# Down projection of a Strassen feed-forward block: product outermost instead of contraction quarter outermost, with the block sums of W2 made ahead, in the attention stage

## The chip, the cores and the metric

One core of a Trainium2 chip runs the whole encoder layer as one program. The metric is the device time of one execution in microseconds (us), lower is better. The engines are named as in the profile: PE (matmul), PEld (its weight load), DVE (vector), ACT (scalar), POOL (GpSimd) and SP, which in this kernel mostly issues DMAs.

## The reference

The layer is a hybrid mixer (Hyena convolutions and a bidirectional mLSTM), a cross-attention and a feed-forward block, over 2048 tokens of width 1024, in fp32. Only the last two matter here:

```python
h = h + _cross_attention(_rms_norm(h, norm_x_g[l]), _rms_norm(mem, norm_mem_g[l]), ...)
h = h + jnp.square(jax.nn.relu(_rms_norm(h, norm_ff_g[l]) @ ff_w1[l])) @ ff_w2[l]   # 1024 -> 4096 -> 1024
return _rms_norm(h, final_norm_g)
```

## The kernel before

**Stages.** In order of time: the input projection with the Hyena filters, Hyena convolutions and mLSTM scan, interleaved by hand (`weave`, L1850); the attention stage (output projection, scores, softmax, value product, four chunks of 512 tokens), which overlaps the last part of the mLSTM; the up projection; the down projection. `TC_ARGS` (L1837) lets a list scheduler set the order of the instructions on every engine when the program is built: an operation with free buffers and ready inputs can be put ahead of others that stand earlier in the text. The result is one instruction stream per engine, SP's stream of DMA issues among them.

**Arithmetic.** An fp32 product is made of three matmuls of a high and a low part (`mm3`, L339 to L341: high by high, low by high, high by low). Each operand tile of 128x512 is therefore split: ACT copies it to the rounded high part (L1521), DVE or POOL subtracts that from the tile to get the low part (L1522, in `halves`). `raw` (L1514) loads such a tile into a ring of six buffers.

**Strassen.** Up and down projection each use seven block products in place of eight (the Winograd form). In the down projection a block of the result is 512 output columns by 512 tokens. `tp` is one of two pairs of token chunks. The contraction runs over 16 tiles of 128 rows in each half of W2's 4096 rows, so there are 16 values `g` of a 2x2 set of 128x512 blocks of W2 (`blocks_of(2, g)`, L1268). The sums of the activation blocks are written to the DRAM tensor `hc` by the up projection.

**Down projection before (L1777 to L1834).** The loop is over four quarters `o` of the contraction, in each over the seven products in `ORDER_DOWN = (1, 6, 7, 5, 3, 2, 4)`, in each over `tp`, in each over the four tiles `k` of the quarter: 28 products x 2 x 4 = 224 steps of 12 matmuls. After four steps a set of four PSUM banks is added into one of 14 SBUF accumulators (`acc`, L1806; copied at L1804 for three products of the first quarter). Three blocks of W2 per `(o, k)` are loaded to `wring` (`load_w`), two sums are made by `sums_w`, a third and fourth in `fetch_a`; all of this, and the residual (`residual`, L1726), is done beside the matmuls, mostly by POOL. In the last quarter the accumulators are combined into the four result blocks (`add`, L1770, on DVE and POOL), which `turned`, `turn` and `finish` transpose, normalise and store.

**Attention before.** In each of the two loops over eight column tiles per chunk (L1382 and L1474), every odd tile takes one entry of the list `sums` (L1322): 20 empty ones and then four calls of `sums_x`, which load four 256 KB tiles of the residual stream, make four block sums of them on POOL and store these. The rest are made in the up projection. In the same loops POOL adds the squares of each row (`ssum`, L1378), on which the statistics of the softmax depend, and DVE splits every weight tile (L344) and every activation (L351).

Of the kernel before, what the change touches and what calls it, by code (L numbers as in the profile page):

```python
# [133 lines left out]
class Prog:  # L134
# [1161 lines left out]

    def attention(self, es):
# [24 lines left out]
        sums = [None] * 20 + list(range(4))  # L1322
# [39 lines left out]
        for c in range(4):  # L1362
# [19 lines left out]
            for ct in range(8):  # L1382
                yield 5.2
                if ct % 2 == 0:
                    w = next(wst)
                else:
                    k = sums.pop(0) if sums else None
                    if k is not None:
                        self.sums_x(A, k, "sm")
# [84 lines left out]
            for ct in range(8):  # L1474
                yield 5.2
                if ct % 2 == 0:
                    w = next(wst)
                else:
                    k = sums.pop(0) if sums else None
                    if k is not None:  # L1480
                        self.sums_x(A, k, "sm")
# [37 lines left out]
    def halves(self, src, tags, bufs, eng):  # L1519
        hi, lo = (self.R.tile([128, 512], F32R, tag=n, name=n, bufs=bufs) for n in tags)  # L1520
        self.nc.scalar.copy(hi, src)  # L1521
        eng.tensor_tensor(lo, src, hi.bitcast(F32), ALU.subtract)  # L1522
        return hi, lo

    def ffn_open(self, es):
        self.R = es.enter_context(self.tc.tile_pool(name="ring", bufs=1, side="right"))
        self.xt = {}
        self.W, self.WD = {}, {}
# [67 lines left out]
    def ffn(self):  # L1596
# [5 lines left out]
        self.C = self.ctx.enter_context(tc.tile_pool(name="wring", bufs=1))  # L1602
# [4 lines left out]
        def fetch_a(n, k):  # L1607
            o, i = prods[n]
            w = self.blocks_of(2, 4 * o + k)
            eng = nc.vector if n < 6 else nc.gpsimd  # L1610
            if i in (6, 7, 5):
                if i == 6:
                    eng.tensor_tensor(self.WD[k, 0], self.WD[k, 2], self.WD[k, 0], ALU.subtract)
                src = self.WD[k, {6: 0, 7: 1, 5: 2}[i]]
            elif i == 1:
                src = self.WD[k, 0]
            else:
                src = self.raw(w[i == 4][1])
                if i == 3:
                    eng.tensor_tensor(src, src, self.WD[k, 0], ALU.subtract)  # L1620
            aq[n, k] = self.halves(src, ("ah", "al"), 4, eng)

        def load_w(o, k):
            w = self.blocks_of(2, 4 * o + k)
            for j, src in enumerate((w[0][0], w[1][0], w[1][1])):
                t = self.WD[k, j] = self.wtile()
                nc.sync.dma_start(out=t, in_=src)

        def sums_w(k, op=nc.gpsimd.tensor_tensor):
            op(self.WD[k, 2], self.WD[k, 1], self.WD[k, 2], ALU.add)  # L1630
            op(self.WD[k, 1], self.WD[k, 0], self.WD[k, 1], ALU.subtract)

        def fetch_b(s, eng=nc.vector):
            n, tp, k = down[s]
            o, i = prods[n]
            bq[s] = self.halves(self.raw(hc[tp, i - 1, 4 * o + k]), ("bh", "bl"), 6, eng)

        with tc.tile_pool(name="up", bufs=1) as U:
# [23 lines left out]
            for n, (tp, g, i) in enumerate(steps):  # L1662
# [7 lines left out]
                if n + 9 >= len(steps) and n + 5 < len(steps):  # L1670
                    load_w(0, n + 9 - len(steps))
# [40 lines left out]
        with tc.tile_pool(name="down", bufs=1) as B:  # L1712
            acc, ms = {}, []
# [6 lines left out]
            for i in (1, 6, 7, 4, 5, 3, 2):  # L1720
                for tp in range(2):
                    acc[i, tp] = B.tile([128, 4, 512], F32, tag="acc", name="acc", bufs=14)
# [3 lines left out]
            def residual(i, tp, k):  # L1726
                n, h = {2: (0, 0), 7: (1, 1), 3: (1, 0), 4: (0, 1)}[i]
                v = acc[i, tp][:, k]
                nc.sync.dma_start(out=v, in_=h2[2 * tp + n, :, 4 * h + k])
                nc.gpsimd.tensor_tensor(v, v, ms[2 * tp + n], ALU.mult)  # L1730
                if i == 4:
                    nc.gpsimd.tensor_tensor(v, v, acc[7, tp][:, k], ALU.subtract)
# [30 lines left out]
            def turned(c, tp, h, i, j, dst=None):  # L1763
                def one(tag, t):
                    turn(c, h, acc[i, tp], acc[j, tp], t, tag)
                    if dst and t == 3:
                        finish(c, dst)
                return [lambda tag, t=t: one(tag, t) for t in range(4)]

            def add(i, j, tp, eng):  # L1770
                for m in range(4):
                    eng.tensor_tensor(acc[i, tp][:, m], acc[i, tp][:, m], acc[j, tp][:, m], ALU.add)

            early = [(i, tp, k) for i in (7, 4, 3, 2) for tp in range(2) for k in range(4)]
            outs = []
            V, G = nc.vector, nc.gpsimd
            for s, (n, tp, k) in enumerate(down):  # L1777
                o, i = prods[n]
                if n == 0 and tp == 0:
                    sums_w(k, nc.vector.tensor_tensor)  # L1780
                if s + 3 < len(down):
                    fetch_b(s + 3, G if s > 199 and k else V)
                if o < 3 and tp == 0 and i == 2:
                    load_w(o + 1, k)
                if o < 3 and tp == 0 and i == 4:
                    sums_w(k)
                if early and s > 3:
                    residual(*early.pop(0))
# [10 lines left out]
                if k < 3:  # L1799
                    continue  # L1800
                for m in range(4):
                    v = acc[i, tp][:, m]
                    if o == 0 and i in (1, 6, 5):
                        nc.scalar.copy(v, bank[m])  # L1804
                    else:
                        d = nc.vector.tensor_tensor(v, bank[m], v, ALU.add)  # L1806
                        if s + 1 == len(down):
                            tc.keep_in_program_order(d)
                if o < 3:
                    continue  # L1810
                if i == 1:
                    add(2, 1, tp, G)
                elif i == 6:
                    add(6, 1, tp, V)
                elif i == 7:
                    add(7, 6, tp, V)
                    add(3, 6, tp, G)
                elif i == 5:
                    add(3, 5, tp, V)
                    add(5, 7, tp, G)  # L1820
                    add(4, 7, tp, G)
                    if tp:
                        outs += turned(1, 0, 1, 5, 1)
                elif i == 3:
                    c = 2 * tp + 1
                    if not tp:
                        outs += turned(3, 1, 1, 5, 1)
                    outs += turned(c, tp, 0, 3, 6, (acc[6, tp], acc[1, tp]))
                elif i == 2:
                    outs += turned(2 * tp, tp, 0, 2, 7)  # L1830
                elif i == 4:
                    outs += turned(2 * tp, tp, 1, 4, 5, (acc[7, tp], acc[5, tp]))
# [116 lines left out]
```

## Time and profile before

| | us |
|---|---|
| median of 3 runs (lowest, highest) | 3226.48 (3220.32, 3226.53) |
| span of the profiled execution, first to last instruction | 3228.4 |
| attention with the end of the mLSTM | about 1240 to 1945 |
| up projection | about 1945 to 2572 |
| down projection, first to last matmul | 2572.6 to 3210.3 |
| tail: last result block | 3210.3 to 3228.4 |

The page gives the profiled execution no time of its own beside its span, which lies 1.9 us above the median of the runs. Rows of the stretches give their length, then busy time and number of instructions of each engine, the granted TensorE clock, the share of time in which the DMA engines are busy, and GB/s. Rows of the timeline give start, length, engine, line, operation, output and inputs; in square brackets stands how long the engine had been idle, and what released it. Rows of groups give count, busy time, mean ns of one, and the idle time ahead of them.

### The profile page before, as it was taken

The page shows a single profiled execution, that of the slowest core. Times are in us where ns is not written, and L with a number is a line of the kernel's source. Part 1 is how long each engine was busy: PE and PEld are TensorE (multiplying, and loading weights), DVE is VectorE, ACT ScalarE, POOL GpSimd, SP SyncE. Part 2 cuts the span into 40 slices and gives each one's busy share as a digit, 9 for nine tenths or more (in the row PEclk, how much of TensorE's full clock was granted, in tenths as well). Part 3 has the DMA queues.
Part 4 walks back from the last instruction along what each step waited for, and adds up shares of the span by engine and source line. Part 5 has one row for each costly group of instructions (what it writes and reads, how often), then busy time and mean ns, then how long its engine had stood idle before and what let it go on. Part 6 is the DMA issues. An engine that isn't in the chain of part 4 may idle for free.

```text
span 3228.4 us, 45284 instructions
## 1 busy us (share of the span) xinstructions
PE 3059.3 (95%) x15241; PEld 2439.5 (76%) x15241; DVE 2034.9 (63%) x3535; ACT 1502.3 (47%) x2873; POOL 1183.0 (37%) x818
## 2 busy tenths in 40 slices
PE   6999999999999876999999998999999999999998
PEld 5655566776668765898979896888788887888876
DVE  7775366345865755777675547656654676556595
ACT  5533366434764343454454445455555543333335
POOL 0122011100121324223151217776756483434483
PEclk9999999999999997999999999999999999999999
DMA  5564776686687988667384537665644474444434
GB/s 189 190 208 161 252 203 201 178 270 182 185 232 206 287 280 283 184 202 243 121 293 126 175 103 246 214 199 177 200 150 154 154 251 153 137 134 150 124 92 167
DMA packets 451777, 617.98 MB, mean 191 GB/s; under 512 B 39631, under 2 KB 247631, under 8 KB 450521
## 3 DMA queue, kind: packets, MB, share of 16 engines
q1 hardware_dynamic: 415412, 556.57, 55.7%
q10 hardware_dynamic: 36132, 58.51, 5.4%
q8 instruction: 121, 1.98, 0.3%
q14 instruction: 112, 0.91, 0.1%
HBM read 416.73 MB, written 198.21 MB: 190 GB/s over the span
## 4 chain that ended last, share of the span: by engine, by line
PE 51%; DMA 7%; DVE 4%; issue 2%; POOL 2%; ACT 1%; SPq 0%; ACTq 0%; POOLq 0%; DVEq 0%
PE mm L341 11%; PE mm L339 11%; PE mm L340 11%; PE hy L341 5%; PE hy L339 5%; PE hy L340 5%; DMA rw<-rows 1%; DVE bl L1522 1%; DMA va<-vd 1%; PE hy L1205 1%; PE hy L1207 1%; DMA wn<-in_xa_wq_t_dram 1%; DMA wr<-xs 1%; DVE wl L344 0%; PE hy L1443 0%
## 5 line engine op out<-in xcount | busy, mean ns | idle before, releaser
L344 DVE TENSOR_TENSOR wl<-wn,wh 128x512 fp32r<-128x512 f32 (+1 forms) x364 | 283.1, 813 | 119.5 <-ACT wh L344 119.3
L1522 DVE TENSOR_TENSOR bl<-wr,bh 128x512 fp32r<-128x512 f32 x213 | 240.9, 1137 | 124.5 <-ACT bh L1521 122.7
L1521 ACT CAST ah<-w 128x512 fp32r<-128x512 f32 x284 | 176.2, 622 | 298.9 <-PE hy L340 153.4
L921 POOL TENSOR_TENSOR b<-b,a 128x512 f32<-128x512 f32 x64 | 87.7, 1371 | 584.6 <-ACT b L919 461.0
L344 ACT CAST wh<-wn 128x512 fp32r<-128x512 f32 (+1 forms) x364 | 208.4, 618 | 193.6 <-PE mm L340 47.0
L339 PE MATMUL mm<-xh,wh 128*128 128x512 f32 x640 | 270.7, 424 | 5.4 <-ACT xh L499 3.2
L1522 DVE TENSOR_TENSOR al<-w,ah 128x512 fp32r<-128x512 f32 x236 | 221.4, 940 | 60.4 <-ACT ah L1521 60.1
L340 PE MATMUL mm<-xl,wh 128*128 128x512 f32 x640 | 257.0, 402 | 1.8 <-DVE xl L344 1.8
L341 PE MATMUL mm<-xh,wl 128*128 128x512 f32 x640 | 258.3, 404 | 0.0
L1521 ACT CAST bh<-wr 128x512 fp32r<-128x512 f32 x232 | 143.7, 621 | 228.8 <-PE mm L341 183.8
L341 PE MATMUL mm<-bh,al 128*128 128x512 f32 x576 | 225.6, 394 | 7.9 <-DVE al L1522 4.7
L339 PE MATMUL mm<-bh,ah 128*128 128x512 f32 x576 | 227.1, 394 | 0.9 <-DVE u L1647 0.8
L340 PE MATMUL mm<-bl,ah 128*128 128x512 f32 x576 | 226.1, 393 | 0.0
L339 PE MATMUL mm<-act,wh 128*128 128x512 f32 x512 | 199.9, 395 | 3.1 <-ACT wh L344 3.1
L340 PE MATMUL mm<-act,wh 128*128 128x512 f32 x512 | 200.8, 392 | 0.0
L341 PE MATMUL mm<-act,wl 128*128 128x512 f32 x512 | 199.6, 393 | 0.3 <-DVE wl L344 0.3
L1378 POOL TENSOR_TENSOR ssum<-ssum,sq 128x512 f32<-128x512 f32 x56 | 81.9, 1462 | 290.8 <-ACT sq L1377 286.4
L339 PE MATMUL hy<-bh,ah 128*128 128x512 f32 x448 | 175.2, 391 | 0.0
L340 PE MATMUL hy<-bl,ah 128*128 128x512 f32 x448 | 174.6, 390 | 0.0
L341 PE MATMUL hy<-bh,al 128*128 128x512 f32 x448 | 174.4, 390 | 0.0
L339 PEld LDWEIGHTS mm<-xh,wh 128*128 128x128 f32 x640 | 121.4, 190 | 65.7 <-issue 29.7
L339 PE MATMUL hy<-xh,ah 128*128 128x512 f32 x384 | 152.1, 396 | 9.3 <-ACT ah L1521 8.5
(367 smaller groups left out, 8742.1 us busy)
## 6 DMA issues: line engine op xcount, KB each, us to landing
wr<-hc SPq DMA_DIRECT2D x224, 256.0 KB
w<-in_ff_w_dram SPq DMA_DIRECT2D x176, 256.0 KB
hc<-t SPq DMA_DIRECT2D x128, 256.0 KB
wn<-in_w_in_dram SPq DMA_DIRECT2D x100, 256.0 KB
hc<-q SPq DMA_DIRECT2D x96, 256.0 KB
fs<-a SPq DMA_DIRECT2D x32, 512.0 KB
a<-fs SPq DMA_DIRECT2D x64, 256.0 KB
a<-zs SPq DMA_DIRECT2D x64, 256.0 KB
```

The lines of the kernel that those rows point to most:

```text
L339: mm(ps, lh, rh, start=start, stop=False)
L340: mm(ps, lh, rl, start=False, stop=False)
L341: mm(ps, ll, rh, start=False, stop=stop)
L344: both = (self.nc.scalar.copy(hi, src), self.nc.vector.tensor_tensor(lo, src, hi.bitcast(F32), ALU.subtract))
L921: nc.gpsimd.tensor_tensor(xt, xt, hi[:, m], ALU.mult)
L1205: nc.tensor.matmul(dst, nm[:, h], va[:, h], start=True, stop=state is None)
L1207: nc.tensor.matmul(dst, rows_[d, 1][:, h], state[:, h], start=False, stop=True)
L1378: nc.gpsimd.tensor_tensor(ssum, ssum, sq, ALU.add)
L1521: self.nc.scalar.copy(hi, src)
L1522: eng.tensor_tensor(lo, src, hi.bitcast(F32), ALU.subtract)
```

## The change

**Loops.** The down projection loops over the seven products alone, each over `tp`, each over all 16 contraction tiles in one set of four banks (224 steps again). The 14 accumulators are gone: `close` runs after each 16 steps, copies or adds the four banks to at most two running blocks (`m1`, `u2`, `u3`, `c22`, ten buffers with the transposed results), and hands a finished result block to `turned`, whose four parts are taken one every third step.

**Operand A.** Every A tile is loaded by `raw`: blocks 11, 12 and 22 of W2 from the input, the four sums from the DRAM tensor `ws`. The split halves of all 16 tiles stay for both `tp`: four in the old ring, twelve in new tiles `dh` and `dl`. The low part is always made on DVE. `load_w`, the old `sums_w` and the subtractions in `fetch_a` are gone.

**Sums of W2.** A new `sums_w(pool, g)` loads four 256 KB blocks, makes four POOL operations and four 256 KB stores. Its 16 calls are put into the attention's list: `sums` is now 4 empty entries, the 16 calls, and the four `sums_x` in their old place.

```diff
+    def sums_w(self, pool, g):
+        op = self.nc.gpsimd.tensor_tensor
+        ws = self.dram("ws", (4, 16, 128, 512))
+        w = self.blocks_of(2, g)
+        t11, t12, t21, t22 = self.four(pool, [w[m][k] for m in range(2) for k in range(2)], "sm")
+        op(t22, t21, t22, ALU.add)
+        op(t21, t11, t21, ALU.subtract)
+        op(t11, t22, t11, ALU.subtract)
+        op(t12, t12, t11, ALU.subtract)
+        for j, t in enumerate((t22, t11, t21, t12)):
+            self.nc.sync.dma_start(out=ws[j, g], in_=t)
...
-        sums = [None] * 20 + list(range(4))
+        sums = [None] * 4 + [partial(self.sums_w, A, g) for g in range(16)] + [partial(self.sums_x, A, i, "sm") for i in range(4)]
...
-        prods = [(o, i) for o in range(4) for i in self.ORDER_DOWN]
-        down = [(n, tp, k) for n in range(len(prods)) for tp in range(2) for k in range(4)]
+        prods = self.ORDER_DOWN
+        down = [(n, tp, k) for n in range(len(prods)) for tp in range(2) for k in range(16)]
...
+        def fetch_a(n, k, *own):
+            w = self.blocks_of(2, k)
+            src = {1: w[0][0], 2: w[0][1], 4: w[1][1], 5: ws[0, k], 6: ws[1, k], 7: ws[2, k], 3: ws[3, k]}[prods[n]]
+            aq[n, k] = self.halves(self.raw(src), *(own or (("ah", "al"), 4, nc.vector)))
...
+            def close(i, tp, bank, last):
+                def plus(dst, role):
+                    for m in range(4):
+                        d = V.tensor_tensor(dst[:, m], bank[m], T[role, tp][:, m], ALU.add)
...
             for s, (n, tp, k) in enumerate(down):
...
                 if s + 3 < len(down):
-                    fetch_b(s + 3, G if s > 199 and k else V)
+                    fetch_b(s + 3)
+                if n == 0 and tp == 0 and k < 12:
+                    fetch_a(0, k + 4, ("dh", "dl"), 12, V, B)
+                if jobs:
+                    jobs.pop(0)()
...
-                    self.mm3(bank[m], ah[:, msl], al[:, msl], bh, bl, k == 0, k == 3)
+                    self.mm3(bank[m], ah[:, msl], al[:, msl], bh, bl, k == 0, k == 15)
                 if tp and n + 1 < len(prods):
-                    fetch_a(n + 1, k)
-                for _ in range(min(len(outs), 2 if len(outs) > 4 or n + 1 == len(prods) else 1)):
-                    outs.pop(0)("mm" if tp else "hy")
+                    fetch_a(n + 1, k, *((("dh", "dl"), 12, V, B) if k > 3 else ()))
+                if outs and k % 3 == 2:
+                    outs.pop(0)("mm" if tp else "hy")
...
+                if k == 15:
+                    close(prods[n], tp, bank, s + 1 == len(down))
```

More of the change, by code (lines that the diff above doesn't have):

```diff
@@ L1386, in attention @@
                 else:
-                    k = sums.pop(0) if sums else None
-                    if k is not None:
-                        self.sums_x(A, k, "sm")
+                    f = sums.pop(0) if sums else None
+                    if f is not None:
+                        f()
                 if c == 0 and ct == 0:
@@ L1478, in attention @@
                 else:
-                    k = sums.pop(0) if sums else None
-                    if k is not None:
-                        self.sums_x(A, k, "sm")
+                    f = sums.pop(0) if sums else None
+                    if f is not None:
+                        f()
                 if c == 3 and ct == 4:
@@ L1517, in raw, with halves @@
         return t
-    def halves(self, src, tags, bufs, eng):
-        hi, lo = (self.R.tile([128, 512], F32R, tag=n, name=n, bufs=bufs) for n in tags)
+    def halves(self, src, tags, bufs, eng, pool=None):
+        hi, lo = ((pool or self.R).tile([128, 512], F32R, tag=n, name=n, bufs=bufs) for n in tags)
         self.nc.scalar.copy(hi, src)
@@ L1527, in ffn_open @@
         self.xt = {}
-        self.W, self.WD = {}, {}
+        self.W = {}
     def ffn_xload(self, tp, i):
@@ L1669, in ffn @@
                     wq.append(self.ffn_w1(*steps[n + 2]))
-                if n + 9 >= len(steps) and n + 5 < len(steps):
-                    load_w(0, n + 9 - len(steps))
                 if n + 2 >= len(steps):
@@ L1712, in ffn @@
         with tc.tile_pool(name="down", bufs=1) as B:
-            acc, ms = {}, []
+            ms = []
             on = [B.tile([128, D], F32, tag="on", name="on", bufs=2) for _ in range(2)]
@@ L1719, in ffn, with block, residual @@
                     ms.append(v)
-            for i in (1, 6, 7, 4, 5, 3, 2):
-                for tp in range(2):
-                    acc[i, tp] = B.tile([128, 4, 512], F32, tag="acc", name="acc", bufs=14)
             gl = B.tile([128, D], F32, name="gl")
             nc.scalar.dma_start(out=gl, in_=a["final_norm_g"].unsqueeze(0).broadcast_to([128, D]))
-            def residual(i, tp, k):
-                n, h = {2: (0, 0), 7: (1, 1), 3: (1, 0), 4: (0, 1)}[i]
-                v = acc[i, tp][:, k]
+            T = {}
+            def block():
+                return B.tile([128, 4, 512], F32, tag="acc", name="acc", bufs=10)
+            def residual(tp, n, h, role, k):
+                own = role == "c22"
+                v = T[role, tp][:, k] if own else B.tile([128, 512], F32, tag="rs", name="rs", bufs=3)
                 nc.sync.dma_start(out=v, in_=h2[2 * tp + n, :, 4 * h + k])
                 nc.gpsimd.tensor_tensor(v, v, ms[2 * tp + n], ALU.mult)
-                if i == 4:
-                    nc.gpsimd.tensor_tensor(v, v, acc[7, tp][:, k], ALU.subtract)
+                dst = v if own else T[role, tp][:, k]
+                nc.gpsimd.tensor_tensor(dst, v, T["u3", tp][:, k] if own else dst, ALU.add)
             ss = B.tile([128, 4, 2, 4], F32, name="ss")
@@ L1761, in finish, with turned @@
                                 in_=dst[h][:, t - 1:t + 1])
-            def turned(c, tp, h, i, j, dst=None):
+            def turned(tp, n, h, role):
+                c = 2 * tp + n
+                dst = T[h, c] = block()
                 def one(tag, t):
-                    turn(c, h, acc[i, tp], acc[j, tp], t, tag)
-                    if dst and t == 3:
-                        finish(c, dst)
+                    turn(c, h, T[role, tp], dst, t, tag)
+                    if (1 - h, c) in T and t == 3:
+                        finish(c, (T[0, c], T[1, c]))
@@ L1768, in turned, with late @@
                 return [lambda tag, t=t: one(tag, t) for t in range(4)]
[L1770 to L1776, printed above, removed]
+            V = nc.vector
+            jobs, outs = [], []
+            def close(i, tp, bank, last):
+                def plus(dst, role):
+                    for m in range(4):
+                        d = V.tensor_tensor(dst[:, m], bank[m], T[role, tp][:, m], ALU.add)
+                        if last:
+                            tc.keep_in_program_order(d)
+                def late(n, h, role):
+                    jobs.extend(partial(residual, tp, n, h, role, k) for k in range(4))
+                if i == 1:
+                    T["m1", tp] = block()
+                    for m in range(4):
+                        nc.scalar.copy(T["m1", tp][:, m], bank[m])
+                elif i == 6:
+                    T["u2", tp] = block()
+                    plus(T["u2", tp], "m1")
+                    late(0, 0, "m1")
+                elif i == 7:
+                    T["u3", tp] = block()
+                    plus(T["u3", tp], "u2")
+                    T["c22", tp] = block()
+                    late(1, 1, "c22")
+                else:
+                    role = {5: "c22", 3: "u2", 2: "m1", 4: "u3"}[i]
+                    plus(T[role, tp], role)
+                    if i == 5:
+                        plus(T["u2", tp], "u2")
+                        late(1, 0, "u2")
+                        late(0, 1, "u3")
+                    outs.extend(turned(tp, i in (5, 3), i in (5, 4), role))
```

73 lines of the change are left out of this document (3 added, 70 removed).

## The prediction

> **What bounds the kernel now.** First the page, then the stages the change touches, by the table of stretches (length, then busy us and instructions of PE, PEld, DVE, ACT, POOL, the granted clock, the DMA share, GB/s).
>
> ```profile
> PE 3059.3 (95%) x15241; PEld 2439.5 (76%) x15241; DVE 2034.9 (63%) x3535; ACT 1502.3 (47%) x2873; POOL 1183.0 (37%) x818
> ```
> ```profile
> 1240.00:1331.00 91.00, 65.49 (x352) 57.31 (x353) 57.14 (x169) 36.20 (x124) 32.75 (x26) 0.81 0.77 242
> 1331.00:1575.00 244.00, 242.37 (x1636) 222.72 (x1635) 178.22 (x474) 122.72 (x344) 75.69 (x56) 1.00 0.65 197
> 1240.00:1575.00 335.00, 307.85 (x1985) 280.04 (x1986) 235.36 (x642) 158.93 (x467) 108.44 (x82) 0.95 0.68 209
> ...
> 2600.00:2680.00 80.00, 75.43 (x323) 61.91 (x323) 67.49 (x55) 31.36 (x55) 74.79 (x47) 0.96 0.74 241
> 2680.00:3100.00 420.00, 420.00 (x1855) 347.77 (x1854) 261.81 (x322) 136.74 (x233) 180.09 (x128) 1.00 0.43 132
> ```
>
> PE is the bound: 95% over the span, 420 of 420 us in most of the down projection, 242 of 244 in the attention. The exception is the start of the attention, where PE is busy 65 of 91 us and the DMA engines 77%. So a change that leaves the matmuls alone can only win where PE waits, and loses wherever it makes PE wait. I read next what PE waited for in the down projection, then the places.
>
> ```profile
> PE mm L341 <- DVE al L1522: 4.6, 1, 4.6
> PE mm L341 <- POOL al L1522: 3.1, 2, 2.9
> ```
> ```profile
> 2661.47 0.39 PE L340 MATMUL mm<-bl,ah 128*128 128x512 f32 x1
> 2666.43 0.79 PE L341 MATMUL mm<-bh,al 128*128 128x512 f32 x1 [4.57 <-DVE al L1522]
> ...
> 2671.24 0.40 PE L340 MATMUL mm<-bl,ah 128*128 128x512 f32 x1
> ...
> 3060.01 0.39 PE L339 MATMUL mm<-bh,ah 128*128 128x512 f32 x1
> ...
> 3062.73 0.39 PE L339 MATMUL mm<-bh,ah 128*128 128x512 f32 x1
> ...
> 3126.09 0.39 PE L340 MATMUL mm<-bl,ah 128*128 128x512 f32 x1
> 3129.39 0.79 PE L341 MATMUL mm<-bh,al 128*128 128x512 f32 x1 [2.91 <-POOL al L1522]
> 3129.98 0.63 PE L339 MATMUL mm<-bh,ah 128*128 128x512 f32 x1
> 3130.40 0.63 PE L340 MATMUL mm<-bl,ah 128*128 128x512 f32 x1
> ...
> 3210.10 0.39 PE L341 MATMUL hy<-bh,al 128*128 128x512 f32 x1
> ```
>
> Twelve matmuls, one step, take 3062.73 - 3060.01 = 2.72 us, 0.227 each. Of 637 us only two real gaps are left, both for the low part of a W2 operand, and after each the next matmuls stand 0.42 apart (3129.98 to 3130.40) and not 0.227.
>
> **The change part by part.**
>
> *Matmuls.* 28 x 2 x 4 x 12 = 2688 before, 7 x 2 x 16 x 12 = 2688 after, with 128 transposes each: no difference.
>
> *What the down projection gains.* The late operand of both gaps hung on sums made beside the matmuls by DVE and POOL (POOL is busy 74.79 of 80 us in the first stretch). These leave the stage, and each A tile is now fetched 16 steps (43.5 us) ahead in place of 4. Gaps: 4.96 + 3.30 less two spacings = 7.8, and the small third one (3.1 - 2.9 = 0.2): 8.0 us. Slow matmuls behind them: 2666.43 to 2671.24 are 11 matmuls in 4.81 us, at full pace 2.49, so 2.3; the same behind the second: 4.6. Last, the tail:
>
> ```profile
> 3209.28 1.68 DVE L1754 TENSOR_SCALAR acc<-acc,or_y 128x512 f32<-128x512 f32 x4
> ...
> 3210.87 2.48 DVE L1806 TENSOR_TENSOR acc<-hy,acc 128x512 f32<-128x512 f32 x4
> ```
>
> The last four additions end at 3213.35 because DVE first scales another chunk's block. PE's last matmul ends at 3210.49; an addition behind it would end at 3211.2. After the change that other block is turned at steps 2 to 11 of the last 16, over 8 us earlier, so 2.1 us go. Together **15 us**. As bounds I take 8 (the gaps alone) and 16.
>
> *What it could lose there.* POOL gives 88 A and 15 B subtractions to DVE, DVE gives up 200 + 24 additions for 56.
>
> ```profile
> L1521 ACT CAST bh<-wr x218: 604/622/681, 2580.5 to 3195.8; 128x512 fp32r<-128x512 f32 x109
> ...
> L1522 DVE TENSOR_TENSOR bl<-wr,bh x203: 673/1090/1825, 2581.1 to 3196.5; 128x512 fp32r<-128x512 f32 x102
> ```
>
> DVE: 336 subtractions at 1.09, 56 additions and 32 turned tiles at about 0.7: 428 us of 622, not the bound. DMA: two 256 KB tiles per step in the second `tp` are 0.524 MB / 2.72 us = 193 GB/s; the first stretch above carried 241. At the start, tiles 4 to 15 of A are made while the product runs. In ACT's new order the copies of tiles 4 to 8 stand behind that of B tile 7, which needs the buffer of step 1, free after 2 x 2.72 = 5.4 us. Tile 4 is ready 0.62 + 1.83 later, at 7.9, needed at 4 x 2.72 = 10.9; behind it the need grows by 2.72 a tile, the work by at most 1.83. I put no loss there. If that cover is gone (a load late by over 3 us), the loss is a gap like the two above, 3 to 7 us.
>
> *What the attention pays.* 16 x 8 = 128 DMAs of 256 KB, 33.55 MB, and 64 POOL operations on two SBUF tiles. In the scheduler's new SP order the first four loads stand right behind the second `acc` load below, 35 of the 128 ahead of the first `gd` weight load, and the last store just ahead of the `vw` loads of the second chunk.
>
> ```profile
> 1243.06 2.57 SPq L1366 DMA_DIRECT2D acc<-in_x_t_dram  x1
> ...
> 1331.18 2.15 SPq L1264 DMA_DIRECT2D wn<-gd  x4
> ...
> 1553.07 3.32 SPq L1264 DMA_DIRECT2D wn<-vw  x4
> ```
>
> So they all fall between about 1243 and 1575, in front of weights, `rows` and `kn` loads that PE needs, and a store that waits for POOL holds what is queued behind it on SP. How full the DMA engines can be is shown by short stretches:
>
> ```profile
> 1240.00:1260.00 20.00, 7.84 (x36) 7.31 (x37) 10.45 (x40) 4.68 (x23) 6.09 (x6) 0.61 0.98 324
> ...
> 1440.00:1480.00 40.00, 38.37 (x192) 32.07 (x191) 24.55 (x58) 23.25 (x63) 20.57 (x16) 1.00 0.92 310
> ...
> 1640.00:1680.00 40.00, 40.00 (x180) 32.94 (x179) 29.76 (x32) 18.79 (x32) 22.42 (x14) 1.00 0.97 328
> 1680.00:1705.00 25.00, 19.49 (x101) 17.82 (x100) 15.89 (x21) 7.91 (x15) 17.20 (x12) 0.80 0.72 221
> 1705.00:1740.00 35.00, 35.00 (x282) 35.00 (x282) 21.77 (x68) 15.64 (x39) 0.00 (x0) 0.95 0.32 98
> ```
>
> 328 GB/s at a share of 0.97 make 338 for a full share. The new bytes need 33.55 MB / 338 = 99 us of it; the stretch already uses 0.68 x 335 = 228. That is 327 of 335 us, a share of 0.98 held for a third of a millisecond. At the best share seen (0.97) the stretch needs 337 us, +2; at 0.90 it needs 363, +28. I take 0.92, the share of the 40 us in which PE still ran almost full: 327 / 0.92 = 355, **+20 us**. Part of it is visible already: in the start of the stage PE's chain runs through the landing of small loads.
>
> ```profile
> 1262.06 3.89 DMA rw<-rows
> ...
> 1290.64 7.07 DMA rw<-rows
> ```
>
> The Trainium skill ("DMA: Bandwidth & Descriptors", section Specifications) gives about 358 GB/s of HBM per core as the limit. No run here reaches it; by that figure, as an estimate, the new bytes would take 94 us, the share would be 0.96 and the cost 5 us less at 0.92.
>
> POOL's operations cost PE something else: DVE.
>
> ```profile
> L1289 POOL TENSOR_TENSOR sm<-sm x4: 1281/1588/1776, 1620.6 to 1697.3; 128x512 f32<-128x512 f32 x4
> ...
> L1292 POOL TENSOR_TENSOR sm<-sm x4: 1271/1604/1755, 1645.5 to 1702.9; 128x512 f32<-128x512 f32 x4
> ```
> ```profile
> 1676.47 0.68 DVE L344 TENSOR_TENSOR wl<-wn,wh 128x512 fp32r<-128x512 f32 x1
> ...
> 1681.01 4.59 DVE L344 TENSOR_TENSOR wl<-wn,wh 128x512 fp32r<-128x512 f32 x3
> ```
> ```profile
> 1690.98 0.39 PE L339 MATMUL mm<-wh,act 128*128 128x256 f32 x1 [2.71 <-ACT act L350]
> ```
>
> The four `sums_x` of the trace show it: while POOL sums, a split takes 4.59 / 3 = 1.53 us in place of 0.68, and at 1688 PE waits for an activation that DVE had held up. The 1680 to 1740 rows lose 5.5 us of PE time, 19.5 x 0.2 = 3.9 to the clock of 0.80 and 35 x 0.05 = 1.8 to that of 0.95: 11.2 us for about four sums, while the 40 us ahead, with 14 POOL operations, lose nothing. So between 0 and 2.8 us per sum, 0 and 45 for 16. The loss coincided with the splits that open the up projection, which the new sums don't meet, so I take the value near the lower row, 0.25 each: **+4 us**.
>
> The Trainium skill ("SBUF — State Buffer", section Who interferes with whom) says that a DVE instruction with two SBUF inputs and a POOL instruction that reads SBUF share a port pair, and the second one waits for the whole of the first. The trace agrees in kind (0.68 against 1.53). Taken at its word for all 64, it is the second rival below.
>
> *Sum.* Against the profiled span: 3228.4 - 15 + 20 + 4 = 3237.4. The median of the runs lies 1.9 lower, so **3235.5 us**.
>
> **Rivals.**
>
> 1. *The sums are hidden* (faster). The scheduler found idle slots for them: POOL is busy 108 of 335 us, PE already idles 25 of the first 91 us, and the stretch from 1640 to 1680 carried 328 GB/s with PE full. It decides by the attention's loss: below 15 - 6.5 = 8.5 us the kernel is faster. At 2 us for DMA and 0 to 5 for DVE, 3226.5 - 15 + 4 = 3215. Against it: PE's idle start is itself bound by landings at 0.98.
> 2. *DVE becomes the attention's bound.* Each of the 64 POOL operations (1.27 to 1.78 us) holds a DVE operation for its whole length: about 64 x 1.5 = 96 us on DVE's 235 of 335, to 331. It is then full on average and late in every burst; at the price of 2.8 us per sum 45 us: 3226.5 - 15 + 45 = 3257.
> 3. *The down projection keeps its gaps*, now at the start of a product, from loads late in a 193 GB/s stream beside the residual's: the gain shrinks to 5, 3245.
> 4. *The two effects cancel*: attention loss of 8.5 to 21, 3220 to 3233.
>
> **How the numbers follow.** Forecast (loss over 21, to about 35) 0.36; rival 1 0.27; rival 2 0.13; rival 3 0.05; rival 4 0.19. What a measurement of this kernel can tell from no change is about 0.2%, 6.5 us. Faster 0.27, same 0.19, slower 0.54. The range runs from rival 1 to rival 2 with its bounds: 3213 to 3260. Inside the likeliest sign alone it would be 3233 to 3248.
>
> **What would show it.** Right: the DMA share between 1240 and 1575 at 0.9 or more, that stretch longer by some 20 us with most of it in its first 100, the last mLSTM steps waiting on `rows`; the down projection from first to last matmul near 624 us with no gap over 1 us, and the last additions within 1 us of the last matmul. Wrong: attention no longer than before (rival 1), `wl` and `act` splits above 1.5 us on average with PE waiting for DVE (rival 2), PE gaps for `al` or `dl` in the down projection (rival 3).

## The result and the profile after

The changed kernel takes 3277.6 us (median of 4 runs, 3273.75 to 3280.45), the kernel before 3226.5 in the same rounds (3220.32 to 3226.97): ratio 1.0172, interval 1.0160 to 1.0184. It is 1.7% slower; 3235.5 was predicted, and the range ended at 3260.

First the page's line of engines after the change, then stretches (columns as in the prediction): the attention from 1240 to the first matmul of the up projection, its two parts, and 400 us of the down projection.

```profile
PE 3081.4 (94%) x15241; PEld 2451.5 (75%) x15241; DVE 1938.0 (59%) x3454; ACT 1496.7 (46%) x2857; POOL 1049.1 (32%) x723
```
```profile
1240.00:1993.36 753.36, 679.81 (x4014) 606.71 (x4015) 478.02 (x1069) 315.14 (x788) 282.32 (x198) 0.93 0.67 217
1240.00:1331.00 91.00, 55.49 (x289) 48.80 (x290) 51.49 (x148) 26.64 (x99) 42.95 (x32) 0.71 0.88 283
1331.00:1600.00 269.00, 241.75 (x1472) 216.77 (x1471) 189.57 (x402) 113.10 (x306) 151.72 (x106) 0.95 0.82 266
2700.00:3100.00 400.00, 400.00 (x1761) 326.00 (x1760) 207.60 (x279) 140.82 (x254) 94.25 (x61) 1.00 0.53 165
```

The same stretch of the kernel before, up to its first up matmul:

```profile
1240.00:1935.15 695.15, 660.74 (x4014) 591.95 (x4015) 446.01 (x1079) 316.19 (x796) 188.29 (x136) 0.97 0.60 188
```

The same 4014 matmuls take 58.2 us longer. 39.1 of that is idle PE time (753.36 - 679.81 = 73.6 against 34.4), and 19.1 is the matmuls themselves (679.81 against 660.74 busy), at a mean granted clock of 0.93 in place of 0.97. By stage, from the first and last matmuls:

| us | before | after |
|---|---|---|
| first up matmul (end of the attention) | 1935.2 | 1993.4 |
| up projection | 637.5 | 631.9 |
| down projection, first to last matmul | 637.5 | 636.1 |
| last matmul to the end of the span | 18.3 | 16.5 |

The down projection lost its gaps: only one wait over 1 us is left (2.05, at 2638.39). But it got only 1.4 us shorter. The timeline of PE shows why. These are the first matmuls of two half products that follow each other (one `tp` of a product, 192 matmuls):

```profile
2760.64 0.39 PE L339 MATMUL hy<-bh,ah 128*128 128x512 f32 x1
...
2805.00 0.39 PE L339 MATMUL mm<-bh,ah 128*128 128x512 f32 x1
```

192 matmuls in 44.36 us are 0.2310 each, where the kernel before had 0.2267. Within the half product, those with weights from `ah` and `al` keep 0.2267, and those from the new tiles `dh` and `dl` take 0.2325: no wait, a slower pace, at a granted clock of 1.00.

### The profile page after: what moved, and what is told of

Its sections match the earlier page's. It is cut to its first block, busy times and chain, and to the rows that moved or that the text cites. A ratio compares the mean times of both kernels' runs of the same rounds, so it can differ in the third digit from the quotient of the medians.

```text
span 3277.9 us, 45342 instructions
## 1 busy us (share of the span) xinstructions
PE 3081.4 (94%) x15241; PEld 2451.5 (75%) x15241; DVE 1938.0 (59%) x3454; ACT 1496.7 (46%) x2857; POOL 1049.1 (32%) x723
## 4 chain that ended last, share of the span: by engine, by line
PE 72%; DMA 13%; DVE 6%; issue 3%; ACT 2%; POOL 2%; SPq 1%; ACTq 0%; DVEq 0%; POOLq 0%
PE mm L339 15%; PE mm L340 15%; PE mm L341 15%; PE hy L341 6%; PE hy L339 6%; PE hy L340 6%; PE hy L176 3%; DMA rw<-rows 2%; PE hy L874 1%; PE mm L843 1%; DVE wl L344 1%; PE hy L916 1%; DMA va<-vd 1%; DMA ws<-sm 1%; DMA sm<-in_ff_w_dram 1%
## 5 line engine op out<-in xcount | busy, mean ns | idle before, releaser
L344 DVE TENSOR_TENSOR wl<-wn,wh 128x512 fp32r<-128x512 f32 (+1 forms) x364 | 296.5, 848 | 106.6 <-ACT wh L344 106.3
L1534 DVE TENSOR_TENSOR bl<-wr,bh 128x512 fp32r<-128x512 f32 x228 | 184.5, 811 | 204.9 <-ACT bh L1533 203.5
L1534 DVE TENSOR_TENSOR al<-w,ah 128x512 fp32r<-128x512 f32 x220 | 202.9, 923 | 57.9 <-ACT ah L1533 57.8
L1533 ACT CAST ah<-w 128x512 fp32r<-128x512 f32 x220 | 136.3, 621 | 208.8 <-PE mm L340 123.9
L340 PEld LDWEIGHTS mm<-xl,wh 128*128 128x128 f32 x640 | 121.1, 189 | 51.9 <-issue 24.2
L339 PE MATMUL mm<-wh,xh 128*128 128x256 f32 (+1 forms) x512 | 152.6, 300 | 5.9 <-ACT st L202 3.4
L341 PE MATMUL hy<-xh,al 128*128 128x512 f32 x384 | 152.2, 396 | 3.5 <-DVE al L1534 3.5
L341 PE MATMUL mm<-wh,act 128*128 128x256 f32 x512 | 148.9, 292 | 5.6 <-DVE act L351 5.6
L339 PE MATMUL mm<-wh,act 128*128 128x256 f32 x512 | 148.7, 292 | 4.0 <-ACT act L350 4.0
L340 PE MATMUL hy<-xl,ah 128*128 128x512 f32 x384 | 151.5, 395 | 1.0 <-POOL xl L1558 1.0
```

The lines of the kernel that those rows point to most:

```text
L339: mm(ps, lh, rh, start=start, stop=False)
L340: mm(ps, lh, rl, start=False, stop=False)
L341: mm(ps, ll, rh, start=False, stop=stop)
L344: both = (self.nc.scalar.copy(hi, src), self.nc.vector.tensor_tensor(lo, src, hi.bitcast(F32), ALU.subtract))
```

## The experiments

**What the attention pays.** Theory A: transfers (their bytes, or their place in SP's queue). Theory B: POOL's additions. Theory C: the order that the scheduler makes. Each kernel below leaves out one thing; all have 4014 to 4041 matmuls in the stage, and the scheduler's order differs in each of them. Each number is from one trace. Three kernels with the changed attention end it at 1992.8 to 1993.5, and four without sums in it at 1937.7 to 1939.8, so differences of 2 us between such traces mean little. Whole executions of the kernel before lie between 3215 and 3236 over all rounds.

*No sums.*

```diff
-        sums = [None] * 4 + [partial(self.sums_w, A, g) for g in range(16)] + [partial(self.sums_x, A, i, "sm") for i in range(4)]
+        sums = [None] * 20 + [partial(self.sums_x, A, i, "sm") for i in range(4)]
-   ... 5: ws[0, k], 6: ws[1, k], 7: ws[2, k], 3: ws[3, k]
+   ... 5: w[1][0], 6: w[1][0], 7: w[1][0], 3: w[1][0]
```

> The block sums of W2 are left out altogether (no loads, no additions, no stores); products 5, 6, 7 and 3 of the down projection read the raw block of W2 in the place of the sum, so the output is not the layer's. All theories of the sums (A: their transfers and the loads queued behind them on SP; B: POOL's additions slowing VectorE; C: the changed order of instructions that comes with them) expect the attention stage to be that of the kernel before: first up matmul at 1935 instead of 1993, span 3220 (3277.9 - 58). If the 58 us have another cause (the renamed slots, the helper's calls), the first up matmul stays near 1993. The down projection keeps its 0.2326 us a matmul and 636 us.

Measured: span 3223.1, first up matmul 1939.1. Nearly the whole loss belongs to the sums (54 of 58 us; three later kernels without them in the attention give 1937.7, 1937.9 and 1939.8).

*Transfers alone, and loads with additions.*

```diff
-        op(t22, t21, t22, ALU.add)
...
-        op(t12, t12, t11, ALU.subtract)
```

> The 64 loads and 64 stores of the block sums stay, the 64 additions on POOL are left out (what is stored is the raw blocks, so the output is not the layer's). Theory A (transfers and the in-order queue of SP): nearly all of the 58 us stay, first up matmul at 1975 to 1995. Theory B (POOL's additions slow VectorE): the loss falls to under 20, first up matmul at 1935 to 1955. A wait of SP's stores for POOL also goes here: if that wait behind the additions is what holds the queue, the loss falls as under B, but VectorE's operations keep their durations.

```diff
-        for j, t in enumerate((t22, t11, t21, t12)):
-            self.nc.sync.dma_start(out=ws[j, g], in_=t)
```

> The 64 loads and 64 additions stay, the 64 stores are left out (products 5, 6, 7 and 3 read the raw block, so the output is not the layer's). Theory A by bytes: half of the 33.5 MB goes, the loss falls to some 25 us, first up matmul near 1960. Theory A by SP's order (stores that wait for POOL block the loads behind them): the loss falls to under 15, near 1945. Theory B: POOL's additions are all there, the loss stays near 58, 1985 to 1995.

Measured: 1962.5 and 1980.2. So neither theory alone: transfers cost 23, the additions on top of them 31. And without the stores 41 remain, so SP's stores that wait for POOL aren't the main thing.

*Additions that don't read.*

```diff
-        op(t22, t21, t22, ALU.add)
...
+        for t in (t22, t21, t11, t12):
+            for _ in range(3):
+                self.nc.gpsimd.memset(t, 0.0)
```

> Each of the 64 additions is replaced by three fills of the same tile with zeros on POOL, which read nothing (the stored sums are zeros, so the output is not the layer's); loads, stores, buffers and their waits are those of the changed kernel. So far the transfers alone cost 23 us of the attention (first up matmul 1962.5 against 1939.1 without sums), the additions another 31 (1993.4). Theory B1 (POOL's reads share a port with VectorE: VectorE's busy time in the attention grew from 454 to 478 us, and PE waits for it): the fills free VectorE, its busy time is back near 455, first up matmul at 1962 to 1972. Theory B2 (POOL's own queue: the sums of squares and the mLSTM's products stand behind additions that wait for loads): the fills hold the queue just as long, first up matmul stays at 1985 to 1995.

Measured: 1975.7, between the two. The stretches up to the first up matmul, with fills (first row) and with transfers alone (second):

```profile
1240.00:1975.70 735.70, 671.80 (x4028) 600.56 (x4026) 451.94 (x1080) 319.13 (x802) 287.88 (x329) 0.95 0.69 225
```
```profile
1240.00:1962.53 722.53, 665.20 (x4039) 594.87 (x4040) 454.33 (x1086) 318.69 (x802) 194.23 (x137) 0.96 0.70 229
```

With POOL held as long as by the additions (287.88 against 282.32 us), VectorE is back at 451.94 from 478.02. So 18 of the 31 us go with what the additions read. The other 13 aren't separated: POOL's own later operations, stores waiting for it, or VectorE after all, since the fills don't free all of it. These are two of its groups between 1240 and 1670 (busy time, mean ns, idle time), each with additions, with fills and with transfers alone:

```profile
L1240 DVE SCALAR_TENSOR_TENSOR ht<-ht,hy,gml 128x128 f32<-128x128 f32 x56 | 28.1, 571 | 0.2
L1240 DVE SCALAR_TENSOR_TENSOR ht<-ht,hy,gml 128x128 f32<-128x128 f32 x56 | 17.8, 389 | 0.2
L1240 DVE SCALAR_TENSOR_TENSOR ht<-ht,hy,gml 128x128 f32<-128x128 f32 x64 | 20.8, 395 | 0.3
```
```profile
L1446 DVE TENSOR_SCALAR e<-e,mx 128x256 f32<-128x256 f32 x32 | 17.5, 548 | 0.5
L1445 DVE TENSOR_SCALAR e<-e,mx 128x256 f32<-128x256 f32 x32 | 17.1, 534 | 0.4
L1442 DVE TENSOR_SCALAR e<-e,mx 128x256 f32<-128x256 f32 x32 | 11.9, 370 | 0.3
```

The fills free `ht`, which has two SBUF inputs (389 ns against 571), and not the softmax's scaling `e` (534 against 548). How VectorE is held can be seen in the changed kernel before its 7.47 us wait at 1421, in the timelines of VectorE, POOL and PE:

```profile
1411.28 6.48 DVE L1240 SCALAR_TENSOR_TENSOR ht<-ht,hy,gml 128x128 f32<-128x128 f32 x8
...
1420.81 0.34 DVE L1446 TENSOR_SCALAR e<-e,mx 128x256 f32<-128x256 f32 x1
```
```profile
1411.47 1.31 POOL L1302 TENSOR_TENSOR sm<-sm 128x512 f32<-128x512 f32 x1 [2.81 <-DMA sm<-in_ff_w_dram]
1412.86 1.27 POOL L1303 TENSOR_TENSOR sm<-sm 128x512 f32<-128x512 f32 x1
1414.21 1.26 POOL L1304 TENSOR_TENSOR sm<-sm 128x512 f32<-128x512 f32 x1
1415.55 1.26 POOL L1305 TENSOR_TENSOR sm<-sm 128x512 f32<-128x512 f32 x1
```
```profile
1413.14 0.60 PE L1455 MATMUL hy<-ident,e 128*128 128x128 f32 x4
1421.20 0.69 PE L1455 MATMUL hy<-ident,e 128*128 128x128 f32 x2 [7.47 <-DVE e L1446]
```

Eight short operations with two SBUF inputs take 6.48 us (2.21 in the kernel with small transfers and no additions, below) while the four additions run. The softmax's `e` stands behind them on VectorE, and PE's next matmul waits for `e`. The Trainium skill ("SBUF — State Buffer", section Who interferes with whom) says that such a VectorE operation contends with a GpSimd operation that reads SBUF and not with one that only writes it; the additions against the fills agree, 478 against 452 us.

The wait itself isn't the additions' alone: at the same place PE waits 6.43 us with transfers alone and 7.22 with small ones. What the kernels with additions have beside it are waits for VectorE like these three of the changed kernel:

```profile
1367.21 0.38 PE L341 MATMUL mm<-wh,act 128*128 128x256 f32 x1 [2.40 <-DVE act L351]
...
1501.84 0.80 PE L1205 MATMUL hy<-va,rw 128*128 128x129 f32 x2 [3.12 <-DVE ht L1240]
...
1580.51 0.39 PE L341 MATMUL mm<-wh,act 128*128 128x256 f32 x1 [2.64 <-DVE act L351]
```

The other three kernels with the additions in this place have 2.21 to 2.62 us at the first and 4.13 to 8.53 at the second; with fills, and with transfers alone, no such wait is over 1 us.

PE pays twice for a wait such as the one at 1421, as the 30 us around it show:

```profile
1410.00:1420.00 10.00, 3.73 (x32) 3.50 (x30) 10.00 (x19) 2.25 (x6) 5.10 (x4) 0.94 0.44 147
1420.00:1430.00 10.00, 8.09 (x53) 7.69 (x54) 8.51 (x25) 5.43 (x14) 0.00 (x0) 0.72 0.84 266
1430.00:1440.00 10.00, 10.00 (x88) 10.00 (x88) 6.21 (x22) 1.19 (x6) 6.20 (x5) 1.00 0.86 279
```

After the wait the granted clock is 0.72 on average over 10 us. The Trainium skill ("TensorE: Matmul & The Clock Gate", section HAM oscillation) gives the rule as no idle gaps above about 3.4 us; the row agrees in kind. Summed over the stage in steps of 2 us, PE's busy time times what the granted clock lacks grows from 16.4 us before to 33.6 after, so by this estimate the clock makes some 17 of the 19.1 us of longer matmuls. It isn't a fixed price of idle time: with transfers alone PE idles 22.9 us more than before (57.3 against 34.4), and its matmuls take only 4.5 longer (665.20 against 660.74).

*Bytes or queue.* Transfers of an eighth of the bytes on SP, then small and full ones issued by POOL:

```diff
-        t11, t12, t21, t22 = self.four(pool, [w[m][k] for m in range(2) for k in range(2)], "sm")
+        t11, t12, t21, t22 = self.four(pool, [w[m][k][0:16] for m in range(2) for k in range(2)], "sm", 16)
...
-            self.nc.sync.dma_start(out=ws[j, g], in_=t)
+            self.nc.gpsimd.dma_start(out=ws[j, g], in_=t)
```

> As the run with the transfers alone (64 loads and 64 stores on SP, no additions), but each moves 16 of the 128 partitions, 32 KB in place of 256 KB; products 5, 6, 7 and 3 read the raw block, so the output is not the layer's. The transfers alone cost 23 us (1962.5 against 1939.1 and 1937.7 for the first up matmul). If that is the bytes (a DMA share of 0.98 to 1.03 in the first 100 us of the stage): under 6 us, 1938 to 1944. If it is SP's order and its eight places for DMAs under way: 15 to 23 stay, 1953 to 1962.

> The small transfers (16 of 128 partitions each, no additions, raw blocks in the place of the sums, so the output is not the layer's), issued on POOL's queue in place of SP's. On SP they cost 19 us of the attention (first up matmul 1957.0 against 1937.7 to 1939.1 without sums). If the cause is SP's order (the mLSTM's small loads stand behind sums' stores that wait for their own loads): 1938 to 1945. If it is the scheduler's new order of the work, or the count of DMAs whatever the queue: 1952 to 1960. If POOL, which now holds the waits, keeps the mLSTM's products behind them: over 1960.

> The full transfers (64 loads and 64 stores of 256 KB, no additions, so the output is not the layer's), issued on POOL's queue in place of SP's. On SP: 1962.5. If SP's order is the cause and the bytes cost the 5 us by which the full transfers exceed the small ones: 1943 to 1950. If the bytes are the cause: 1958 to 1966. If POOL's queue becomes the place of the wait: over 1966.

Measured, with the first matmul of the output projection (`mm<-act`, soon after 1240) beside the first up matmul:

| | first `mm<-act` | first up matmul |
|---|---|---|
| no sums in this stage (four kernels) | 1291.5 to 1297.1 | 1937.7 to 1939.8 |
| small on SP / on POOL | 1294.4 / 1296.1 | 1957.0 / 1950.0 |
| full on SP / on POOL | 1304.4 / 1307.3 | 1962.5 / 1967.8 |

At the first `mm<-act` the full transfers are 10.0 and 11.2 us later than the small ones (1304.4 - 1294.4, 1307.3 - 1296.1), though kernels without sums differ by 5.6 there; at the first up matmul 5.5 on SP and 17.8 on POOL. The DMA engines were nearly full at that start: their share between 1240 and 1331 is 0.99 with full transfers on SP, 0.82 with small ones. So by these differences the bytes cost some 5 to 18 us. From the first `mm<-act` to the first up matmul the kernels without sums take 640.6 to 646.9 us (mean 644.7), those with transfers 653.8 to 662.7: another 9 to 18 us, whatever the size. VectorE's waits (total, times, longest), without sums and with small transfers on SP, between 1240 and 1670, show one way that it may arise:

```profile
DVE ve L1076 <- DMA va<-vd: 11.6, 5, 4.7
```
```profile
DVE ve L1076 <- DMA va<-vd: 28.7, 6, 13.0
```

And the timelines of SP and VectorE around that 13.0 in the small transfers' kernel:

```profile
1379.26 3.71 SPq L1303 DMA_DIRECT2D ws<-sm  x4
1383.01 1.81 SPq L1280 DMA_DIRECT2D sm<-in_ff_w_dram  x4
1384.87 1.28 SPq L1303 DMA_DIRECT2D ws<-sm  x2
...
1393.09 0.53 SPq L1068 DMA_DIRECT2D va<-vd  x1
```
```profile
1385.67 0.42 DVE L1437 TENSOR_REDUCE mx<-mm 128x1 f32<-128x256 f32 x1
1399.13 0.70 DVE L1076 TENSOR_TENSOR ve<-va,cols 128x516 f32<-128x516 f32 x1 [13.04 <-DMA va<-vd]
...
1404.73 2.21 DVE L1240 SCALAR_TENSOR_TENSOR ht<-ht,hy,gml 128x128 f32<-128x128 f32 x8
```

A load that the mLSTM needs is issued behind the sums' DMAs and some other loads (not shown). VectorE sits idle for it, with the softmax behind; PE goes on meanwhile, and waits 7.22 us for `e` at 1411.71. It isn't the only way: with full transfers on SP the longest wait for `va` is 3.7 us, and PE's for the softmax is 6.43 all the same. (The last row is the price of eight `ht` operations without additions on POOL, used above.) On POOL's queue the longest such wait is 4.1 us, but POOL is then busy 252 us in place of 188. How much of the 9 to 18 us is the queue and how much the scheduler's order stays open.

**The pace of the down projection.** The small tile `ss` lies ahead of `dh` and `dl`. Widened:

```diff
-            ss = B.tile([128, 4, 2, 4], F32, name="ss")
+            ss = B.tile([128, 512], F32, name="ss")[:, 0:32].rearrange("p (c h t) -> p c h t", c=4, h=2)
```

> The changed kernel with the one small tile in front of the down stage's resident tiles (ss, 128 bytes a partition) widened to 2048 bytes, so that the resident operand tiles dh and dl begin at the same offset within 2048 bytes as every other matmul operand of the kernel. Theory D (offset sets the pace): matmuls on dh and dl fall from 0.2326 to 0.2268 us, the down projection from 636.3 to 624.6, span 3266. Rival (the pace comes from elsewhere, such as the place of the tiles or the share of other engines' traffic): no change, 636 and 3278. Attention stays at +58 either way.

Measured: span 3267.4, attention unchanged (1993.5), down projection 625.1, the granted clock 1.00 here too. The half product of above, now 43.52 us:

```profile
2758.78 0.39 PE L339 MATMUL hy<-bh,ah 128*128 128x512 f32 x1
...
2802.30 0.39 PE L339 MATMUL mm<-bh,ah 128*128 128x512 f32 x1
```

Then offsets that differ from each other (`ss` of 256 numbers, a tile of 320 between `dh` and `dl`):

> The changed kernel, all of its work, with dh moved by 896 bytes and dl by 2176, so that they begin at 992 and 224 within 2048 bytes a partition, in place of 96 and 96; every other weight tile of the kernel begins at 2016. 992 and 2016 are the same within 1024 bytes, 224, 992 and 2016 within 256, 96 is like 2016 only within 128. So if the pace goes by 2048: both stay at 0.2326 us. By 1024 or 512: dh at 0.2268, dl at 0.2326. By 256: both at 0.2268, and the down projection falls by 11 us to 625. If the offset has nothing to do with it and it was the moving of the tiles as such, both fall too, which this run can't tell from 256.

Measured: span 3265.9, down projection 625.0; every plain half product takes 43.52 us, `dh` and `dl` both run at 0.2267. So 992, 224 and 2016 (all 224 within 256) are fast, 96 is slow. These offsets are read off the allocation, not off a trace; the edits themselves show that `dh` and `dl` became fast when moved by 1920, 896 or 2176 bytes, each of which is 128 more within 256. All five kernels with the wide `ss` give 625.1 to 626.8, all eight with the narrow one 636.1 to 637.8. An offset of 96 set by any other means, and others within 256, weren't tried.

**Is there a gain at all?** No sums, aligned tiles:

> No block sums of W2 (products 5, 6, 7 and 3 read the raw block, so the output is not the layer's) and the aligned dh and dl: the most that the new loop order can give if the sums cost nothing. The two measured effects add: attention end at 1939, up 632, down 625, tail 16, span 3212, against 3223.1 without sums alone and 3228.4 of the kernel before: 0.3 to 0.5% faster than the kernel before. If it isn't faster, the new order has no gain to give, wherever the sums are made.

Measured: 3214.0 (ratio 0.9953, 0.9937 to 0.9969). The new loop order is worth 0.5% if the sums cost nothing; this kernel leaves them out. So where can they be made? In the up projection (16 calls, half the additions on VectorE), and late in the attention (calls later in the list, loads held back by a POOL operation that reads the third chunk's sums of squares):

```diff
+                if i == 2 and wsum and (g in (6, 8, 10, 12) if tp == 0 else g > 1):
+                    self.sums_w(U, wsum.pop(0))
```

> All of the layer's work. Aligned dh and dl, and the sums moved into the up projection: 16 calls over its groups from the seventh of the first token pair on, two of four operations on VectorE and two on POOL, in four own buffers that exist only in that stage. POOL is busy about 434 of 632 us there and VectorE 385, the DMA share is 0.57. Theory of the cause (bursts of loads at the start of the attention, and POOL's operations beside a late VectorE): the up projection has room for both, so it costs 0 to 10 us: span 3212 to 3222, at or under the kernel before. Rival (POOL or the loads of W1 behind the sums' stores on SP become late in the up projection): up grows by 15 to 40, span 3227 to 3252.

```diff
+            if hold is not None:
+                self.nc.gpsimd.tensor_tensor(x[:, 0:1], hold, hold, ALU.add)
             self.nc.sync.dma_start(out=v, in_=src)
```

> All of the layer's work. Aligned dh and dl; the sums stay in the attention but are held back until the first sums of squares of the third chunk (about 1700 us), by one small POOL operation per tile that reads them, when the mLSTM has ended, POOL is idle and the DMA share is 0.3 to 0.4. The same loads, additions and stores as in the changed kernel. If the cost is that of the place (transfers into a full DMA queue, additions beside the mLSTM's chain through VectorE): first up matmul at 1939 to 1955, span 3212 to 3228. If it is that of the operations themselves wherever they stand in the attention: 1980 to 1995, span 3255 to 3267.

Measured: 3254.9 (ratio 1.0079, 1.0058 to 1.0100) and 3238.1 (1.0038, 1.0025 to 1.0050). The rival held in the up projection: it takes 672.5 us in place of 632, with sixteen waits for `al`, 27.6 us together and 3.8 the longest. Late in the attention the cost falls to 22 us (1959.5), a little over what was expected of a pure matter of place: new waits came for `ym` loads (6.43) and `ssum` (4.79).

The stage with room was the down projection itself: POOL 94 of 400 us, DMA share 0.53, A tiles needed 16 steps later. Two products on raw blocks now come first, two of the four sums are made on the way and never stored, so 32 stores remain of 64 (a further change of the running blocks isn't shown).

```diff
-    ORDER_DOWN = (1, 6, 7, 5, 3, 2, 4)
+    ORDER_DOWN = (1, 2, 6, 7, 5, 3, 4)
...
+            if prods[n] in (7, 3):
+                y = sw(w[1][0] if prods[n] == 7 else ws[1, k])
+                nc.gpsimd.tensor_tensor(x, x, y, ALU.subtract)
...
+                if 12 <= s < 60 and s % 3 == 0:
+                    sums_w(s // 3 - 4)
```

> All of the layer's work. Aligned dh and dl, no sums of W2 in the attention; they are made in the down projection itself, where POOL has become idle and the DMA share is 0.55. For that the order of the products is 1, 2, 6, 7, 5, 3, 4 (two products on raw blocks first, 174 us), the sums for products 6 and 5 are made in steps 12 to 57 of the first 64 (three loads, two POOL operations, two stores every third step), those for 7 and 3 on the way (one load and one POOL operation more per tile). If the attention's place was what cost, and the down projection hides this: attention end 1938, down 625, span 3212 to 3218, faster than the kernel before by 0.3 to 0.5%. If sums cost PE wherever they stand (as 36 us in the up projection, 22 in the late attention): 3230 to 3250.

Measured: 3211.6 us against 3224.9 for the kernel before (ratio 0.9961, 0.9948 to 0.9974). This does all of the work and beats both kernels, the kernel before by 0.4%. Its stretches, attention and down projection:

```profile
1240.00:1937.86 697.86, 660.10 (x4015) 591.10 (x4015) 446.55 (x1077) 316.10 (x793) 188.00 (x136) 0.97 0.59 187
2569.68:3196.51 626.83, 623.40 (x2801) 515.51 (x2799) 355.48 (x452) 229.77 (x413) 207.60 (x132) 1.00 0.64 210
```

VectorE is busy 355 of 627 us, and PE idles 3.4 us.

## Why the prediction was wrong, step by step

From 3237.4 for the span to the measured 3277.9 are 40.5 us.

- *POOL's operations, "I take the value near the lower row, 0.25 each: +4 us".* This is the step that failed most: 31 us, 1.9 per sum, of which 18 go with what the additions read, which holds VectorE, and 13 with POOL being held or whatever else the fills leave. The upper row, 2.8, was nearer. The reason given, that the new sums don't meet the splits that open the up projection, was true (the last of their additions starts at 1601.6) and didn't matter: earlier in the stage they hold other VectorE operations, `act` and `ht`, for which PE waits too. The second rival had the contention right and its size wrong: 26 us of VectorE time (478 against 452) and not 96, and VectorE was busy 189.57 of 269 us where the sums run, so it was not the bound.
- *Matmuls, "no difference".* The count was right, the duration not: 2016 of them on tiles at a new offset, 11.0 us (636.1 against 625.1). No row of the trace before had such a tile.
- *Transfers, "+20 us".* Measured 23. The size was right, in part by luck, for the cause was right only in part: small transfers, with the DMA share hardly raised, cost 17 to 19 us on SP all the same. The share that was forecast is there where the transfers stand alone, and is missed with the additions (first row transfers alone, second the changed kernel, with the same bytes):

```profile
1240.00:1575.00 335.00, 284.95 (x1763) 255.80 (x1764) 220.11 (x571) 145.58 (x424) 109.32 (x79) 0.92 0.91 301
1240.00:1575.00 335.00, 274.88 (x1574) 243.42 (x1574) 225.14 (x510) 132.90 (x379) 178.14 (x127) 0.88 0.84 273
```

With small ones on SP it is 0.69, with no sums 0.68. (The best share in the prediction's own rows was 0.98, not 0.97; nothing hangs on it.)
- *The gain of the down projection.* Right once the pace is taken out: 637.5 to 625.1 is 12.4, predicted 12.6 (8.0 and 4.6). The tail gained 1.8, predicted 2.1. The one gap left is 2.05 us, where none over 1 was forecast.
- *Not foreseen:* the up projection is 5.6 us shorter, and takes 631.2 to 634.2 in every kernel that lacks the old W2 loads at its end, save the one with sums in it; why wasn't tried. Without sums the attention still ended 4 us later than in the profile before (1939.1 to 1935.2; 2.5 to 4.7 in the four such kernels); why stays open.

Together: POOL 26.8 (30.8 - 4), transfers 3.4, the attention without sums 4.0, up -5.6, pace 11.0, gaps 0.2, tail 0.3, and 0.3 for 14.7 rounded to 15: 40.4.

## What to carry to other kernels

Work moved to an idle engine is priced by what it holds up there: which operations of another engine slow down beside it, what stands behind it on each engine, and how near those stand to PE. Put it where the consumer has slack for it, not where the engine's busy share is low; here the sums cost 54 us early in the attention, 40 in the up projection (half of them on VectorE), 22 late in the attention and next to nothing in the stage that uses them, with half of the stores (ratio 0.9961, against 0.9953 with no sums at all, in other rounds). And when tiles move, look at the spacing of matmuls without waits, not only at gaps.

## What the runs showed of the hardware that was not expected

- Weight tiles that begin, by the allocation, at 96 within 256 bytes a partition run 128x512 fp32 matmuls at 0.2325 us each, at 224 within 256 at 0.2267: 2.6%, with no wait in the trace.
- Idle PE time can cost about half as much again, mostly through the granted clock: 39.1 us idle, 19.1 us of longer matmuls. With transfers alone it was a fifth: 22.9 and 4.5.
- POOL operations that only write (fills) left `ht`, with two SBUF inputs, at 389 ns, but `e` took 534 in place of 370.
- 128 DMAs of 32 KB each cost the stage 17 to 19 us on SP's queue (1957.0 against 1937.7 to 1939.8), where those of 256 KB cost 23 to 25 (1962.5).
